# Two gate blocks of layer 2's modulation, from TensorE in the attention to VectorE in the scans

## Chip, cores and metric

One Trainium2 chip, one core. A core has five engines that run at the same time, each through its own list of instructions in order: TensorE (PE, matrix products into PSUM), VectorE (DVE), ScalarE (ACT), GpSimd (POOL) and SyncE (SP, which here only starts transfers). The profile shows the loading of a product's fixed operand as a row of its own (PEld). The metric is the time of one execution in microseconds (us); less is better. Inputs and outputs are float32.

## What is computed

Two layers on 256 latent tokens and 256 context tokens of width 2048: first two kinds of attention side by side, then a gated DeltaNet. In each, a vector `c` for the latent tokens and one, `c_ctx`, for the context tokens become a shift, a scale and a gate through the weights `w_mod`.

```python
def adaln_params(cond, w_mod, b_mod):
    return jnp.split(jax.nn.silu(cond) @ w_mod + b_mod, 3, axis=-1)

def modulate(x, gain, shift, scale):
    return rmsnorm(x, gain) * (1 + scale) + shift
...
def deltanet_layer(x, ctx, c, c_ctx, w_mod, b_mod, norm, w_in, conv_w, a_log, dt_bias, o_norm, w_out, update_ctx):
    sh, sc, gt = adaln_params(c, w_mod, b_mod)
    sh_c, sc_c, gt_c = adaln_params(c_ctx, w_mod, b_mod)
    qx, kx, vx, zx, gx, bx = deltanet_inputs(modulate(x, norm, sh[:, None], sc[:, None]) @ w_in, conv_w, a_log, dt_bias)
    qc, kc, vc, zc, gc, bc = deltanet_inputs(modulate(ctx, norm, sh_c, sc_c) @ w_in, conv_w, a_log, dt_bias)
...
    x = x + gt[:, None] * deltanet_out(o_xf + flip_t(o_xb), zx, o_norm, w_out)
    if update_ctx:
        ctx = ctx + gt_c * deltanet_out(o_cf + flip_t(o_cb), zc, o_norm, w_out)
    return x, ctx
...
        x, ctx = deltanet_layer(x, ctx, c, c_ctx, dn_w_mod[j], dn_b_mod[j], dn_norm[j], dn_w_in[j], dn_conv[j],
                                dn_a_log[j], dn_dt_bias[j], dn_o_norm[j], dn_w_out[j], update_ctx)
    return rmsnorm(x, final_norm)
```

The second layer is the last, so `update_ctx` is false there: its gate is used for the latent tokens alone, after the scans.

## The kernel before

**Modulation.** The 6144 columns of `w_mod` (2048 rows) are cut into 12 blocks of 512 columns, 4 MB each; `mods[l]` holds the result for both vectors (two samples, column 0 for `c`, column 1 for `c_ctx`). In layer 2 (`l` = 1) blocks 0 to 3 are the shift, 4 to 7 the scale, 8 to 11 the gate. Two helpers compute a block:

- `adaln` (L121) on TensorE: 16 products `pmod` (L141) of the weights `mraw` with `cond`, four at a time in different columns of the array, a copy to `macc` on VectorE (L147), four transposes `pmt` (L150), and small sums into `mods`.
- `adaln_lanes` (L161) on VectorE: for each of the 16 slices of 128 rows and each sample, a multiply-add of 128x512 into `lacc` (L175 for the first slice, L177 after it), 32 in all; then 8 small products `pml` with ones (L184) that sum over the partitions. Two accumulators, one per sample, take turns.

Both load through the buffers `mraw` of one pool, three of them at this place, 512 KB each, and `lacc` is one buffer.

**Stages.** Layer 1 runs through a first attention (neighbourhood, seven heads and an eighth later) and a latent one (eight heads), then the output projection `mm<-gx` (16 units of 48 products, L90 to L92). Up to the end of layer 1's work the order of every engine is made by a scheduler: it follows the order of the code as a priority, and starts early what is free to start. A head is `attend` (L367): scores `sp`, maximum (L389), exponential, reciprocal (L394) and scaling (L395), transposes `pt`, the split `PT` (L358), the product `po` (L365), and `goA` and `goB` (L405), whose second closes a head.

Layer 2's blocks 2, 3 and 8 are stepped through during the latent heads on TensorE (L472), block 9 after them (L495). The latter's products are kept behind the last product of the last head's projections (`issue_after`, L139). Blocks 4 to 7 follow on VectorE (L512), and 10 and 11 on TensorE at the change of layers (L522). They all pass through the same three `mraw` buffers in this order.

**The scans.** Layer 2's scans over chunks (L1220 on) run in an order written out by hand for PE, DVE and ACT: 70 steps `st` from -2 to 69. A step carries one step of the context's scan (`C`) and, six steps behind, one of the latent tokens' (`X`), and up to step 57 one weight tile of 128x1024 for the values (24 products of 512 columns). `hi` (L1125) loads weight tiles into four buffers `raw`, three ahead, and casts one on ACT (L1131); `lo` (L1134) makes the rest `wlo` on DVE (L1139). In a scan step PE makes `pks` (L1033), DVE makes `R` from it (L1037), PE makes `ptr` from R (L1045). Every second step ends, on DVE, with two conv taps (L585) in front of the next step's R; every fourth has the gated output (L1111) there too. `project` (L632) uses the gate, from step 58 on.

Of the kernel before, what the change touches and what calls it, by code (L numbers as in the profile page):

```python
# [8 lines left out]
F32 = mybir.dt.float32  # L9
F32R = mybir.dt.float32r  # L10
AF = mybir.ActivationFunctionType
ALU = mybir.AluOpType
# [4 lines left out]
KT = 16  # L17
# [9 lines left out]
def trunk_kernel(ctx: ExitStack, tc: tile.TileContext, g):  # L27
# [16 lines left out]
    def cst(name, shape, src=None):  # L44
        t = const.tile(shape, F32, name=name, tag=name)
        if src is not None:
            nc.scalar.dma_start(t, src)
        return t
# [14 lines left out]
    ab_bmod, dn_bmod = vecs[:, 56:104], vecs[:, 104:152]  # L63
    o_gain = vecs[:, 152:153]
    mods = [cst(f"mod{l}", [128, 48, 2]) for l in range(2)]
    Am = [cst(f"Am{l}", [128, KT, 2]) for l in range(2)]


    def load_raw(src, n=1024):
        raw = wp.tile([128, 1024], F32, name="raw", tag="raw", bufs=4)  # L70
        nc.sync.dma_start(raw[:, :n], src)
        return raw
# [88 lines left out]
    def adaln_lanes(l, ps, pm, tp, chunks, after=None):  # L161

        wm, bmod, gain = ((g["ab_wm"], ab_bmod, ab_gain), (g["dn_wm"], dn_bmod, dn_gain))[l]
        for ch in chunks:
# [26 lines left out]
                V.tensor_tensor(Am[l][:, f], Am[l][:, f], gain[:, f].unsqueeze(2).broadcast_to([128, 4, 2]), op=ALU.mult)  # L191
            yield

    def steps(it, n=1000):
        for _ in range(n):
            if next(it, it) is it:
                break
# [62 lines left out]
    with tc.tile_pool(name="s0", bufs=2) as tp, tc.tile_pool(name="s0p", bufs=1, space=PSUM) as ps:  # L260
        V.memset(cond, 0.0)
        A.activation(cond[:, :, 0:2], cc, AF.Silu)
        xs = ((xA, g["xT"]), (xB, g["cT"]))
        for j in range(0, KT, 4):
            for x, src in xs:
# [53 lines left out]
    with tc.tile_pool(name="ab", bufs=2, reuse_waits="tile") as tp, \  # L319
            tc.tile_pool(name="abp", bufs=2, space=PSUM, reuse_waits="tile") as ps:  # L320
        u, last_mm = NS, None
        mr = tc.alloc_tile_pool(name="mr", bufs=2)

        def later(pool, parts, after=None):
            for l, chunks, lanes in parts:
                if lanes:
                    yield from adaln_lanes(l, ps, "pm", pool, chunks, after)
                else:
                    yield from adaln(l, ps, ("pm", "pm"), pool, [(4 * ch, 4) for ch in chunks], after=after)
# [139 lines left out]
                V.tensor_tensor(ch[:, 8 + j], craw[:, j], ch[:, j].bitcast(F32), op=ALU.subtract)  # L469
        cr.release()  # L470
        mr = tc.alloc_tile_pool(name="mr2", bufs=2, reuse_waits="tile")
        ahead = later(mr, ((1, (2, 3, 8), 0),))  # L472

        rows = slice(0, 64), slice(64, 128)
        attend(*na7)
# [16 lines left out]
            attend(*o, 8 + h, None, ([qr[:, 2 * h + i] for i in range(2)], [kr[:, i] for i in range(2)]))  # L492

        steps(ahead)
        steps(later(mr, ((1, (9,), 0),), last_mm))  # L495
        pace = 0
        gx = parts_tile("gx")
        gh, gl = gx[:, 0], gx[:, 1]
# [141 lines left out]
    with tc.tile_pool(name="dn", bufs=2, reuse_waits="tile") as tp, \  # L640
# [356 lines left out]
        def load(kh, s):  # L997
            o = Head()
            o.s, o.kh = s, kh
            n = 4 if s == 0 else 2  # L1000
            o.kq, o.kt = kq[s][kh % 2], kt[s][kh % 2]
            nc.sync.dma_start(o.kq, spk[kh][:, 512 * s:512 * s + 128 * n].rearrange("p (s t) -> p s t", t=128))
            nc.sync.dma_start(o.kt, spt[kh][:, 256 * s:256 * s + 256].rearrange("p (s t) -> p s t", t=128))
            u0 = (kh % 2) * 8 + s * 4
            o.ub = zb[s][kh % 2]
            blocks(o.ub, spu[kh // 2][:, :, u0:u0 + 4])
            if s == 0:
                o.ab = zb[2][kh % 2]
                blocks(o.ab, spt[kh][:, 512:1024].rearrange("p (a u i) -> p a u i", a=2, i=64))
                o.ot = ots[kh % 2]  # L1010
            return o
# [110 lines left out]
        W += [g["dn_wo"][u][:, 1024 * c:1024 * c + 1024] for u, c in wo_order]  # L1122
        raws, wt = [], []

        def hi():  # L1125
            j = len(wt)
            if j < len(W):
                while len(raws) < min(len(W), j + 3):
                    raws.append(load_raw(W[len(raws)]))
                h = wp.tile([128, 1024], F32R, name="whi", tag="whi", bufs=3)  # L1130
                A.copy(h, raws[j])  # L1131
                wt.append([h])
# [22 lines left out]
        def nothing():  # L1155
            return iter(())
# [59 lines left out]
        outs = early()  # L1216
        GATES = {56: (0, 4, 8), 57: (12, 16), 58: (20,), 66: (24,)}
        LAG = 6
        fins = nothing()
        for st in range(-2, 64 + LAG):  # L1220
            i, n = st // 4, st % 4
# [66 lines left out]
                take(fins, 1)  # L1288
            if vals and st % 2 == 1:
                prev = cur  # L1290
            for k in GATES.get(st, ()):
                gate(k, 4)
            if st == 68:
# [146 lines left out]
```

## Time and profile before

| | us |
|---|---|
| median of 3 runs | 2491.8 |
| lowest and highest | 2489.74, 2504.61 |
| the profiled execution, from outside | 2493.04 |
| its span, from first to last instruction | 2491.2 |
| TensorE busy in the span | 2428.2 (97%) |
| VectorE busy | 1762.8 (71%) |

A row of a group or of the timeline has the line in the code, the engine, the operation, what it writes <- what it reads, the shape, xcount for the number of instructions merged, and what the engine waited for before it in brackets. Matmul times include their way through the array, so neighbours overlap. L90 to L92 are the three products of a split float32 multiplication.

The busy times by slice of a fortieth of the span, in tenths, show where VectorE is loaded; counted from 1, the latent heads lie in slices 12 to 15, the output projection in 15 to 18, the scans in 28 to 38:

```profile
PE   6999999999989999999999999999999999999998
DVE  4654678883356687856998988885777777777765
DMA  8872645542253366664665666774343333336454
```

### The profile page before, as it was taken

Reading aid. Unit: us, or ns where it says so; the run is one execution under the profiler, and the core shown is the slowest. Engines: PE = TensorE matmul, PEld = TensorE weight load, DVE = VectorE, ACT = ScalarE, POOL = GpSimd, SP = SyncE. Lnnn points to the kernel's source line nnn. Section 1 sums busy time; section 2 is a strip of 40 time slices with the busy share of each in tenths; the row PEclk is TensorE's granted clock in tenths of the full one; section 3 lists DMA queues with packets and bytes.
Section 4 is the critical chain, followed back from the end, with each engine's and each line's share of the span. In section 5 each row is a group of like instructions: output and inputs, shape, how many; then the busy total and the mean of one; then the engine's idle time right before and its main releaser. Section 6 shows DMA issues by size and latency. Waiting matters only on the chain.

```text
span 2491.2 us, 42483 instructions
## 1 busy us (share of the span) xinstructions
PE 2428.2 (97%) x16110; PEld 1963.1 (79%) x16110; DVE 1762.8 (71%) x3538; ACT 1105.6 (44%) x2446; POOL 161.1 (6%) x165
## 2 busy tenths in 40 slices
PE   6999999999989999999999999999999999999998
PEld 4557888888858878858998989987777777777787
DVE  4654678883356687856998988885777777777765
ACT  4223332333254432257565655634444544445453
POOL 0000000000000000020011101000000000012000
PEclk9999999999999999999999999999999999999999
DMA  8872645542253366664665666774343333336454
GB/s 252 282 277 87 200 154 172 169 157 84 88 187 110 102 198 204 226 210 136 195 173 158 179 178 180 204 201 108 87 116 103 115 112 98 106 100 184 148 193 141
DMA packets 254940, 397.24 MB, mean 159 GB/s; under 512 B 122257, under 2 KB 163857, under 8 KB 254609
## 3 DMA queue, kind: packets, MB, share of 16 engines
q1 hardware_dynamic: 253584, 393.00, 52.0%
q8 instruction: 127, 2.08, 0.3%
q10 hardware_dynamic: 1152, 1.54, 0.2%
q14 instruction: 77, 0.62, 0.1%
HBM read 356.94 MB, written 35.39 MB: 157 GB/s over the span
## 4 chain that ended last, share of the span: by engine, by line
PE 88%; issue 5%; DMA 3%; DVE 2%; ACT 1%; SPq 0%; POOL 0%; DVEq 0%; POOLq 0%; ACTq 0%
PE mm L90 21%; PE mm L91 20%; PE mm L92 20%; PE pks L1033 3%; PE pmod L141 3%; PE ptr L1045 2%; PE sp L365 2%; PE mm L105 2%; PE po L365 1%; DMA mraw<-dn_wm 1%; PE ptr L1078 1%; PE psu L1064 1%; PE pks L1064 1%; PE pt L398 1%; PE mm L107 1%
## 5 line engine op out<-in xcount | busy, mean ns | idle before, releaser
L90 PE MATMUL mm<-hx,whi 128*128 128x512 f32 (+1 forms) x2304 | 843.7, 366 | 2.3 <-ACT t L664 2.2
L91 PE MATMUL mm<-hx,whi 128*128 128x512 f32 (+1 forms) x2304 | 820.6, 356 | 2.5 <-issue 2.5
L92 PE MATMUL mm<-hx,wlo 128*128 128x512 f32 (+1 forms) x2304 | 819.4, 356 | 0.6 <-DVE wlo L78 0.6
L77 ACT CAST whi<-raw 128x1024 fp32r<-128x1024 f32 (+2 forms) x346 | 338.6, 980 | 701.4 <-PE mm L91 502.3
L78 DVE TENSOR_TENSOR wlo<-raw,whi 128x1024 fp32r<-128x1024 f32 (+2 forms) x346 | 394.3, 1142 | 204.3 <-ACT whi L77 198.2
L90 PEld LDWEIGHTS mm<-hx,whi 128*128 128x128 f32 x2304 | 438.8, 190 | 106.3 <-issue 27.0
L92 PEld LDWEIGHTS mm<-hx,wlo 128*128 128x128 f32 x2304 | 438.6, 190 | 65.1 <-issue 4.2
L91 PEld LDWEIGHTS mm<-hx,whi 128*128 128x128 f32 x2304 | 438.8, 190 | 61.4 <-issue 9.2
L177 DVE SCALAR_TENSOR_TENSOR lacc<-mraw,cond,lacc 128x512 f32<-128x512 f32 x300 | 208.6, 746 | 0.7 <-DMA mraw<-dn_wm 0.7
L585 DVE SCALAR_TENSOR_TENSOR acc<-cin,taps,acc 128x508 f32<-128x508 f32 (+3 forms) x256 | 187.2, 731 | 20.3 <-ACT acc L576 17.2
L105 PE MATMUL mm<-hx,whi 128*128 128x512 f32 x480 | 173.1, 404 | 0.1
L1055 DVE SCALAR_TENSOR_TENSOR vl<-ptr,egm,vh 128x128 fp32r<-128x128 f32 x224 | 64.7, 346 | 95.1 <-ACT rf L1052 37.9
L107 PE MATMUL mm<-hx,wlo 128*128 128x256 f32 x457 | 128.4, 281 | 1.3 <-DVE wlo L1139 1.2
L141 PE MATMUL pmod<-mraw,cond 128*32 128x512 f32 (+2 forms) x640 | 98.4, 508 | 28.1 <-DMA mraw<-ab_wm 18.8
L1139 DVE TENSOR_TENSOR wlo<-raw,whi 128x1024 fp32r<-128x1024 f32 x84 | 102.5, 1221 | 13.5 <-ACT whi L1131 13.4
L105 PEld LDWEIGHTS mm<-hx,whi 128*128 128x128 f32 x480 | 88.9, 188 | 24.5 <-issue 5.0
L816 DVE SCALAR_TENSOR_TENSOR outer<-L,bv,X 128x31 f32<-128x31 f32 (+15 forms) x248 | 99.4, 401 | 6.4 <-POOL X L811 0.5
L90 PE MATMUL mm<-gx,whi 128*128 128x512 f32 x256 | 100.3, 394 | 3.4 <-DVE x1B L515 2.4
L599 ACT ACTIVATE ac<-acc 128x128 f32<-128x128 f32 x160 | 37.4, 300 | 144.2 <-DVE acc L585 144.1
L91 PE MATMUL mm<-gx,whi 128*128 128x512 f32 x256 | 100.4, 392 | 0.5 <-DVE gx L503 0.5
L92 PE MATMUL mm<-gx,wlo 128*128 128x512 f32 x256 | 99.8, 391 | 0.0
L1049 ACT ACTIVATE vh<-ptr,egm 128x128 fp32r<-128x128 f32 x224 | 71.3, 374 | 57.1 <-PE ptr L1045 55.2
(301 smaller groups left out, 3648.5 us busy)
## 6 DMA issues: line engine op xcount, KB each, us to landing
raw<-dn_w SPq DMA_DIRECT2D x194, 512.0 KB
mraw<-dn_wm SPq DMA_DIRECT2D x96, 512.0 KB
mraw<-ab_wm SPq DMA_DIRECT2D x88, 512.0 KB
raw<-ab_w SPq DMA_DIRECT2D x66, 512.0 KB
raw<-dn_wo SPq DMA_DIRECT2D x64, 512.0 KB
raw<-ab_wo SPq DMA_DIRECT2D x32, 512.0 KB
raw<-ab_w SPq DMA_DIRECT2D x32, 256.0 KB
spt<-sp SPq DMA_DIRECT2D x64, 128.0 KB
```

The costliest lines, as they stand in the source:

```text
L77: A.copy(hi[:, :m], raw[:, :m])
L78: V.tensor_tensor(lo[:, :m], raw[:, :m], hi[:, :m].bitcast(F32), op=ALU.subtract)
L90: PE.matmul(ps, wh[:, c], xh[:, k0 + k, sl], start=first and k == 0, stop=False)
L91: PE.matmul(ps, wh[:, c], xl[:, k0 + k, sl], start=False, stop=False)
L92: end = PE.matmul(ps, wl[:, c], xh[:, k0 + k, sl], start=False, stop=last and k == kt - 1)
L105: PE.matmul(p2, wh[:, c], x[:, :, k0 + k], start=start, stop=stop)
L107: PE.matmul(p2[:, 0], wl[:, c], x[:, 0, k0 + k], start=False, stop=False)
L141: PE.matmul(pmod[32 * q:32 * q + 32, :m], cond[:, 4 * kg + q, :], raw[c // 1024][:, half + c % 1024:half + c % 1024 + m], start=kg == 0, s ...
L177: V.scalar_tensor_tensor(acc[:, s], raw[:, q], cond[:, k, s:s + 1], acc[:, s], op0=ALU.mult, op1=ALU.add)
L585: V.scalar_tensor_tensor(o3[:, :, i0:i1], p3[:, :, i0 + d:i1 + d], taps[:, ch, t:t + 1], o3[:, :, i0:i1], op0=ALU.mult, op1=ALU.add)
L816: V.scalar_tensor_tensor(o, L[:, rows, k:k + 1].broadcast_to([128, n, m]), bv[:, k:k + 1], X[:, k:k + 1, cols].broadcast_to([128, n, m]), ...
L1139: V.tensor_tensor(w, raws[j], h.bitcast(F32), op=ALU.subtract)
```

## The change

Blocks 8 and 9 are no longer computed by `adaln` in the attention. A new helper, `lanes`, computes them on VectorE during the scans, for the latent tokens' sample alone (`n` = 1), one weight tile of two slices per step, from step 5 to step 20; the first load is issued in step 4. Each tile takes two multiply-adds, both on the same accumulator, which lies in a free part of `room["e"]`. Its loads use the `raw` buffers of the scans' weights, so `hi` looks only two tiles ahead (`depth`) while it lasts. `cond` does not live as long as the scans, so column 0 is copied to `cond1` at the start. After each eighth tile, four products with ones sum over the partitions.

```diff
@@ -63,6 +63,7 @@
     mods = [cst(f"mod{l}", [128, 48, 2]) for l in range(2)]
+    cond1 = cst("cond1", [128, KT, 1])
     Am = [cst(f"Am{l}", [128, KT, 2]) for l in range(2)]
@@ -191,6 +192,35 @@
+    def lanes(l, chunks, acc_of, cnd, n, pt_of):
+        wm, bmod = ((g["ab_wm"], ab_bmod), (g["dn_wm"], dn_bmod))[l]
+        tiles = [(ch, t) for ch in chunks for t in range(8)]
+        load = lambda ch, t: load_raw(wm[ch, t // 2][:, t % 2 * 1024:t % 2 * 1024 + 1024])
+        ahead = load(*tiles[0])
+        yield
+        for i, (ch, t) in enumerate(tiles):
+            raw, ahead = ahead, load(*tiles[i + 1]) if i + 1 < len(tiles) else None
+            if t == 0:
+                acc = acc_of(ch)
+            for q in range(2):
+                k = 2 * t + q
+                for e in range(n):
+                    x = raw[:, 512 * q:512 * q + 512]
+                    if k == 0:
+                        V.tensor_scalar(acc[e], x, cnd[:, k, e:e + 1], None, op0=ALU.mult)
+                    else:
+                        V.scalar_tensor_tensor(acc[e], x, cnd[:, k, e:e + 1], acc[e], op0=ALU.mult, op1=ALU.add)
+            yield
+            if t == 7:
+                pt = pt_of(n)
+                for j in range(4):
+                    for e in range(n):
+                        PE.matmul(pt[:, j, e:e + 1], acc[e][:, j * 128:j * 128 + 128], ones[:, 0:1], start=True, stop=True)
+                f = slice(4 * ch, 4 * ch + 4)
+                V.tensor_tensor(mods[l][:, f, :n], pt, bmod[:, f].unsqueeze(2).broadcast_to([128, 4, n]), op=ALU.add)
@@ -260,6 +290,7 @@
         A.activation(cond[:, :, 0:2], cc, AF.Silu)
+        A.copy(cond1, cond[:, :, 0:1])
@@ -469,7 +500,7 @@
-        ahead = later(mr, ((1, (2, 3, 8), 0),))
+        ahead = later(mr, ((1, (2, 3), 0),))
@@ -492,7 +523,6 @@
         steps(ahead)
-        steps(later(mr, ((1, (9,), 0),), last_mm))
@@ -1122,10 +1152,13 @@
+        depth = 3
         def hi():
             j = len(wt)
             if j < len(W):
-                while len(raws) < min(len(W), j + 3):
+                while len(raws) < min(len(W), j + depth):
@@ -1216,6 +1249,9 @@
         LAG = 6
+        gates = lanes(1, (8, 9), lambda ch: [room["e"][:, 3072 + 512 * (ch % 2):3584 + 512 * (ch % 2)]], cond1, 1,
+                      lambda n: ps.tile([128, 4, n], F32, name="pml", tag="tr", bufs=1))
@@ -1288,6 +1324,10 @@
+            if st == 3:
+                depth = 2
+            if 4 <= st < 56:
+                depth = 2 if next(gates, 0) is None else 3
             for k in GATES.get(st, ()):
```

The order of the instructions changes at three places. Lines after the change are some 30 higher than before (L177 is L178 there, L405 is L436, L1037 is L1067).

The first is the list of PE where the last latent head is worked on, from its last projections on; before the change:

```order
L92 MATMUL mm<-cx,wlo 128x512
L141 MATMUL pmod<-mraw,cond 32x512 x5
L398 MATMUL pt<-ident,pr 128x128 x2
L141 MATMUL pmod<-mraw,cond 32x512
L365 MATMUL sp<-kT,qT 128x512
L365 MATMUL po<-PT,vt 128x256
L365 MATMUL sp<-kT,qT 128x512 x3
L365 MATMUL sp<-kr,cx 128x512 x3
L365 MATMUL sp<-kT,qT 128x512
L365 MATMUL po<-PT,vt 128x256 x11
```

and after it:

```order
L93 MATMUL mm<-cx,wlo 128x512
L396 MATMUL sp<-kT,qT 128x512 x2
L396 MATMUL sp<-kr,cx 128x512 x3
L396 MATMUL po<-PT,vt 128x256
L396 MATMUL sp<-kT,qT 128x512 x3
L396 MATMUL sp<-kr,cx 128x512 x3
L396 MATMUL po<-PT,vt 128x256 x11
L429 MATMUL pt<-ident,pr 128x128 x4
L396 MATMUL sp<-kT,qT 128x256 x3
L396 MATMUL sp<-kr,cx 128x256 x3
L185 MATMUL pml<-ones,lacc 128x1
L396 MATMUL po<-PT,vt 128x256
```

Block 9's `pmod` are gone, and `pml`, the sums of a block that VectorE computed (one of 4 to 6), now stands within the head.

The second is the list of VectorE in one of the latent heads, behind the `goB` that closes the head ahead of it; before:

```order
L405 TENSOR_TENSOR goB<-po,goB 128x256
L358 TENSOR_TENSOR vt<-pv,vt 128x512
L389 TENSOR_REDUCE mx<-sp 128x1
L358 TENSOR_TENSOR PT<-pt,PT 128x4x128
L389 TENSOR_REDUCE mx<-sp 128x1
L361 SCALAR_TENSOR_TENSOR qT<-mm,qT 128x512
L394 RECIPROCAL rc<-sm 128x1
L395 TENSOR_SCALAR pr<-pr,rc 128x256
L78 TENSOR_TENSOR wlo<-raw,whi 128x512
L358 TENSOR_TENSOR kT<-mm,kT 128x512
L147 COPY macc<-pmod 128x512
```

and after:

```order
L436 TENSOR_TENSOR goB<-po,goB 128x256
L192 TENSOR_TENSOR Am_87<-Am_87,vecs 128x8
L389 TENSOR_TENSOR vt<-pv,vt 128x512
L389 TENSOR_TENSOR PT<-pt,PT 128x4x128
L425 RECIPROCAL rc<-sm 128x1
L178 SCALAR_TENSOR_TENSOR lacc<-mraw,cond,lacc 128x512 x2
L426 TENSOR_SCALAR pr<-pr,rc 128x256
L79 TENSOR_TENSOR wlo<-raw,whi 128x1024
L420 TENSOR_REDUCE mx<-sp 128x1
L178 SCALAR_TENSOR_TENSOR lacc<-mraw,cond,lacc 128x512 x3
L389 TENSOR_TENSOR PT<-pt,PT 128x4x128
L425 RECIPROCAL rc<-sm 128x1
```

Multiply-adds of blocks 4 to 6 (L177 before, L178 now) stand between the head's own instructions; before the change none stands in the first seven latent heads.

The third is in the scans, at the end of an even step with the gated output; VectorE before:

```order
L1083 TENSOR_TENSOR rf<-rf,ptr 128x256
L585 SCALAR_TENSOR_TENSOR acc<-cin,taps,acc 128x2x254 x2
L1111 SCALAR_TENSOR_TENSOR re<-pot,ngain,re 128x512
L1037 SCALAR_TENSOR_TENSOR R<-pks,neg,vx_17131 128x128 x2
L1037 SCALAR_TENSOR_TENSOR R<-pks,neg,vc 128x128 x2
L1055 SCALAR_TENSOR_TENSOR vl<-ptr,egm,vh 128x128 x2
```

and after:

```order
L1113 TENSOR_TENSOR rf<-rf,ptr 128x256
L615 SCALAR_TENSOR_TENSOR acc<-cin,taps,acc 128x2x254 x2
L1141 SCALAR_TENSOR_TENSOR re<-pot,ngain,re 128x512
L214 SCALAR_TENSOR_TENSOR re<-raw,cond_85,re 128x512 x2
L1067 SCALAR_TENSOR_TENSOR R<-pks,neg,vx_17049 128x128 x2
L1067 SCALAR_TENSOR_TENSOR R<-pks,neg,vc 128x128 x2
L1085 SCALAR_TENSOR_TENSOR vl<-ptr,egm,vh 128x128 x2
```

The two multiply-adds of `lanes` (L214) come between the conv taps and the next step's R. On SP's queue at such a place, before:

```order
L71 DMA raw<-dn_w 128x1024
L993 DMA rc<-spt_8931 64x8x64
L995 DMA rc<-spt_8931 64x4x64
L1003 DMA rf<-spt_8932 128x256
L71 DMA raw<-dn_w 128x1024
L1002 DMA kq_16903<-spk_8917 128x256
```

and after:

```order
L72 DMA raw<-dn_w 128x1024
L1023 DMA rc<-spt_8849 64x8x64
L1025 DMA rc<-spt_8849 64x4x64
L72 DMA raw<-dn_wm 128x1024
L1033 DMA rf<-spt_8850 128x256
L72 DMA raw<-dn_w 128x1024
L1032 DMA kq_16821<-spk_8835 128x256
```

A load of the modulation's weights (`dn_wm`) stands between two loads of the scans' weights (`dn_w`), ahead of the loads of a head's keys.

## The prediction

> **What bounds the kernel now.** I read the page's first lines, then a table of windows by stage, then the chain of waits in order of time.
>
> ```profile
> span 2491.2 us, 42483 instructions
> PE 2428.2 (97%) x16110; PEld 1963.1 (79%) x16110; DVE 1762.8 (71%) x3538; ACT 1105.6 (44%) x2446; POOL 161.1 (6%) x165
> ```
>
> TensorE (PE) is busy for 97% of the span, but such a share hides stages with different limits. The windows below give, per stretch, its length and then the busy time of PE, weight loads (PEld), VectorE (DVE) and ScalarE (ACT). The first is the first latent head with what leads up to it, the second the next six heads, the third one of these six that has no modulation work in it, the fourth the last head, the fifth the output projection.
>
> ```profile
> 719.88:766.18 46.30, 44.40 (x225) 31.12 (x224) 28.16 (x57) 20.59 (x40) 0.00 (x0) 1.00 0.56 184
> 766.18:873.81 107.63, 107.63 (x615) 85.90 (x615) 65.48 (x142) 47.89 (x109) 0.00 (x0) 1.00 0.33 104
> 838.36:854.84 16.48, 16.48 (x96) 14.22 (x95) 10.60 (x24) 7.74 (x19) 0.00 (x0) 1.00 0.20 65
> 873.81:901.31 27.50, 27.04 (x134) 21.06 (x133) 25.90 (x62) 14.37 (x42) 0.00 (x0) 1.00 0.50 156
> 901.31:1066.00 164.69, 161.28 (x729) 133.80 (x730) 130.74 (x199) 40.70 (x61) 0.00 (x0) 0.99 0.68 217
> ```
>
> A plain head takes 16.48 us, PE never idle, VectorE working 10.60 of it. So PE sets the heads, and VectorE has 5.9 us to spare in each. The projection is PE's too (161.28 of 164.69).
>
> The scans come next: the chain of waits passes the same product, pks, again and again.
>
> ```profile
> 1771.61 1.45 PE pks L1033 x12
> ...
> 1810.60 1.45 PE pks L1033 x12
> ...
> 2005.52 1.45 PE pks L1033 x12
> ...
> 2044.50 1.45 PE pks L1033 x12
> ```
>
> ```profile
> 2000.00:2100.00 100.00, 100.00 (x625) 77.44 (x623) 73.15 (x191) 48.36 (x154) 7.93 (x8) 1.00 0.38 107
> ```
>
> 1810.60 − 1771.61 = 38.99 us for four steps, and 2044.50 − 2005.52 = 38.98 much later: the scans tick with PE, 9.75 us a step, and in the window above VectorE works 73.15 of 100 us. A microsecond taken from PE in the heads or put on it in the scans counts in full, unless another engine takes over as the bound.
>
> **Part 1, blocks 8 and 9 leave TensorE.** Busy time of the instructions on pmod (first two rows) and on pmt (last two), in windows around each block:
>
> ```profile
> 755.00:795.00 40.00, 5.09 (x32) 0.85 (x32) 0.69 (x1) 1.00 0.43 139
> 858.00:880.00 22.00, 7.81 (x32) 1.23 (x32) 0.69 (x1) 1.00 0.65 211
> ...
> 755.00:810.00 55.00, 0.60 (x4) 0.50 (x4) 0.19 (x1) 1.00 0.38 122
> 858.00:880.00 22.00, 0.60 (x4) 0.47 (x4) 0.00 (x0) 1.00 0.65 211
> ```
>
> PE is freed of 5.09 + 7.81 + 0.60 + 0.60 = 14.1 us, VectorE of 0.69 + 0.69 + 0.19 = 1.6. All of it lies in the heads, on the path.
>
> **Part 2, what the diff does not say.** Blocks 4 to 7 were computed on VectorE, as multiply-adds into lacc, nearly all in the output projection, since block 9 kept the mraw buffers until the last head's projections were issued. Without it the scheduler pulls them into the heads. Counted in the order of VectorE from one goB row to the next, the multiply rows (L175, L177) in the eight latent heads go from 0, 0, 0, 0, 0, 0, 0, 13 to 22, 14, 14, 14, 4, 18, 12, 15, that is 100 more.
>
> ```profile
> L177 DVE SCALAR_TENSOR_TENSOR lacc<-mraw,cond,lacc x300: 730/746/754, 280.2 to 1063.4; 128x512 f32<-128x512 f32 x150
> ...
> 911.39 2.73 DVE L177 SCALAR_TENSOR_TENSOR lacc<-mraw,cond,lacc 128x512 f32<-128x512 f32 x4
> ```
>
> One lasts 746 ns, but four in a row take 2.73 us, since each starts before the one ahead has ended: (2.73 − 0.746) / 3 = 0.66 us apart. A head with 14 of them asks VectorE for 10.60 + 14 × 0.66 = 19.8 us against PE's 16.48: the bound changes engine. Over all eight heads VectorE needs 28.16 + 65.48 + 25.90 + 100 × 0.66 − 1.6 = 183.9 us, where the stretch now takes 46.30 + 107.63 + 27.50 = 181.43. It cannot be busy throughout: the head with 4 multiplies needs 10.60 + 2.64 = 13.2 us of it, 3.2 below the plain head's 16.48, and the first stretch 28.16 + 22 × 0.66 = 42.7, some 2.4 below the 45.1 that is left of 46.30 without a quarter of block 8 (5.09 / 4). So 183.9 + 5.6 = 189.5 us, **8.1 us longer**. From below: if the order lets all multiplies hide, PE's own work is left. The sums of blocks 4 to 6 over the partitions (pml) move along with them:
>
> ```profile
> 940.88 1.68 PE pml L184 x16
> ```
>
> 44.40 + 107.63 + 27.04 − 14.1 + 3 × 1.68 = 170.0 us, with today's 2.4 us of waits 172.4, or 9.0 shorter. From above: the multiplies stand inside the softmax sequence of an engine that works in order, so each may delay what PE waits for next; wholly serial that is 181.4 − 14.1 − 1.6 + 66.0 = 231.7 us, 50 longer. I take the busy sum: the plain head's row shows 5.9 us of idle time to fill, which the serial end denies.
>
> The Trainium skill, "VectorE: DVE Perf Modes", section "The DRAIN you can't avoid", says that an operation does not start until the pipe has emptied, and that one that is not held may start earlier. By its first half the hundred would cost 74.6 us in place of 66.0, and the sum would be 8.6 us higher; by the 2.73 us row the second half holds here.
>
> **Part 3, the output projection.** Three of its four sums over partitions are gone from PE: 3 × 1.68 = **5.0 us shorter**, as PE is its bound. VectorE's 130.74 us there lose the multiplies, which gains nothing more.
>
> **Part 4, the multiplies in the scans.** For one sample there are 2 per tile, one tile a step, at the end of steps 5 to 20. Both write the same accumulator, so they do not overlap; two such rows are the conv taps (L585), 1.53 us. Rows around the end of an even step, with the products ptr that need R:
>
> ```profile
> 1771.99 1.53 DVE L585 SCALAR_TENSOR_TENSOR acc<-cin,taps,acc 128x508 f32<-128x508 f32 x2
> ...
> 1773.95 0.60 DVE L1037 SCALAR_TENSOR_TENSOR R<-pks,neg,vc 128x128 f32<-128x128 f32 x2
> ...
> 1775.60 0.61 PE L1045 MATMUL ptr<-R,ra 128*128 128x128 f32 x4
> ...
> 1781.34 0.42 DVE L1083 TENSOR_TENSOR rf<-rf,ptr 128x256 f32<-128x256 f32 x1 [1.06 <-PE ptr L1078]
> ...
> 1782.36 0.61 DVE L1037 SCALAR_TENSOR_TENSOR R<-pks,neg,ra 128x128 f32<-128x128 f32 x2 [0.60 <-PE pks L1033]
> ...
> 1782.89 0.60 DVE L1037 SCALAR_TENSOR_TENSOR R<-pks,neg,vc 128x128 f32<-128x128 f32 x2
> ...
> 1785.29 0.61 PE L1045 MATMUL ptr<-R,ra 128*128 128x128 f32 x4
> ...
> 1813.59 0.60 DVE L1037 SCALAR_TENSOR_TENSOR R<-pks,neg,vc 128x128 f32<-128x128 f32 x2
> ...
> 1814.59 0.61 PE L1045 MATMUL ptr<-R,rb 128*128 128x128 f32 x4
> ```
>
> After an even step R is done at 1774.55 and used at 1775.60, 1.05 us later. The new pair stands ahead of R in VectorE's queue, so PE waits 1.53 − 1.05 = 0.48 us. Where the gated output (L1111) is in the queue too, R is done at 1814.19 and used at 1814.59: 1.53 − 0.40 = 1.13 us. After an odd step R waits 0.60 us for pks anyway and has 1.80 us to spare: nothing. Eight even steps, three with L1111: 5 × 0.48 + 3 × 1.13 = 5.8 us. The sums over partitions are half as many for one sample: 2 × 0.84 = 1.7 us of PE. Together **7.5 us longer**. Bounds: 1.7 (all waits absorbed) and 16 × 1.13 + 1.7 = 19.8.
>
> **Part 5, SP's queue and the rest.** Sixteen loads of 512 KB leave the heads and sixteen come in the scans, so SP issues as many. There they share the four raw buffers, so the lead of the weight loads falls from three tiles to two.
>
> ```profile
> 1778.78 0.33 SPq L71 DMA_DIRECT2D raw<-dn_w  x1
> ...
> 1813.41 1.03 ACT L1131 CAST whi<-raw 128x1024 fp32r<-128x1024 f32 x1
> ...
> 895.99 8.21 DMA mraw<-dn_wm
> ...
> 2240.90 4.02 DMA re<-god
> ```
>
> The load of 1778.78 is cast at 1813.41 (the fourth cast after it): 34.6 us of lead, less two steps of 9.75 makes 15.1. Loads of that size were waited for 8.21 us in the busy projection, 4.02 in the scans: still hidden. Behind a modulation load that waits for VectorE stand kt, rf and the next weights, but what it waits for was done a step earlier. POOL gets nothing. The copy of cond1 falls on ACT, idle for 56% of the span: nothing.
>
> **Sum.** 8.1 − 5.0 + 7.5 = +10.6 us. The profiled execution took 2493.0 us, 1.2 above the median of the three runs, 2491.8; so the median should come to 2502.4, call it **2502 us**, 0.4% longer. About 1%, 24.9 us, is what a measurement of this kernel can tell from no change.
>
> **Rivals.**
> *The heads stay with PE.* VectorE's 5.9 spare microseconds and the early weights hide all multiplies: −9.0 − 5.0 + 7.5 = −6.5, 2485 us. Against it stands 19.8 above 16.48. 0.20.
> *The scans swallow the pairs.* VectorE is idle for 27 of 100 us there, and the waits are shorter than I count: 8.1 − 5.0 + 1.7 = +4.8, 2497 us. Against it: the idle time lies after R, not before. 0.08.
> *No overlap on VectorE.* With a queue that is never empty, each multiply costs its full 746 ns: 100 × 0.746 − 66.0 = 8.6 us on top of the forecast's +10.6, so +19.2 and 2511 us. This is the first half of the Trainium skill's rule in "VectorE: DVE Perf Modes"; the trace speaks against it. 0.08.
> *The softmax becomes serial*, slower by over 1%. In the heads PE's order is fixed, a late softmax row holds all behind it, and VectorE in turn waits for PE. Half-way to the serial end, (189.5 + 231.7) / 2 = 210.6 us, the heads cost 29.2 more and the sum is 29.2 − 5.0 + 7.5 = +31.7, 2524 us. It decides from some 204 us on, where heads with 14 multiplies last over 22 us. For it: multiplies stand between maximum and reciprocal. Against it: a head of the first attention carries such rows already, VectorE 33.87 of 38.88 us busy and PE still never idle:
>
> ```profile
> 418.25:457.13 38.88, 38.88 (x200) 32.92 (x199) 33.87 (x61) 12.46 (x22) 0.00 (x0) 1.00 0.53 174
> ```
>
> 0.14.
> *Weights come late in the scans.* Where a load takes over 15.1 us each step waits; at 17 us, 16 × 1.9 = 30.4 more than the forecast, 2533 us. Twice the longest wait shown: 0.03.
>
> **Chances and range.** The forecast has the rest, 0.47, with its own range from 2496 to 2510. For 8 in 10 the range runs from 2484, where the first rival ends, to 2522, which leaves out half of the serial case and the late weights. Faster by over 1% (below 2467) is out of reach of every case: 0.01. Slower by over 1% (above 2516.7): the serial case mostly and the late weights, 0.16. Within 1%: 0.83.
>
> **What would show it.** In the profile after: goB rows of the heads with 14 multiplies about 19.8 us apart, with PE now waiting there for VectorE's rows; if they stay at 16.5, part 2 is wrong. The projection about 5 us shorter. In the scans the distance of 38.99 us grows by about 1.6 to 1.9 for steps 5 to 20, with PE's waits in front of ptr and released by R; after step 21 it is 38.99 again. Weight casts that wait for a DMA would overthrow part 5. The forecast as a whole is wrong if the heads take under 180 or over 204 us.

## The result, and the profile after

| | before | after |
|---|---|---|
| median (7 runs each) | 2492.38 us | 2509.79 us |
| lowest and highest | 2489.74, 2504.61 | 2507.82, 2513.91 |
| the profiled execution | 2493.04 us | 2509.56 us |
| its span | 2491.2 us | 2507.7 us |

The ratio is 1.0064, with a 95% interval of 1.0047 to 1.0082: 0.6% longer, a small difference, but the interval lies clear of 1. The forecast was 2502 us, 10.6 longer; the medians stand 17.4 apart.

The page's first lines, after the change:

```profile
span 2507.7 us, 42402 instructions
PE 2429.8 (97%) x16054; PEld 1965.6 (78%) x16054; DVE 1776.0 (71%) x3566; ACT 1107.9 (44%) x2449; POOL 156.3 (6%) x165
```

Almost nothing moves in the totals. The totals hide the change; the table of windows shows it. Columns as before: the stretch and its length, then the busy time of PE, PEld, VectorE (DVE), ScalarE, GpSimd, then the granted clock, the DMA share and GB/s. The first row of the kernel after is the first latent head with what leads up to it, the second the four heads behind it, the third one of these four (14 multiplies), the fourth the next two, the fifth the last head, the sixth the projection up to the first product of block 10.

```profile
720.49:776.56 56.07, 51.99 (x250) 37.15 (x249) 43.19 (x85) 23.43 (x46) 0.00 (x0) 0.97 0.56 183
776.56:850.65 74.09, 68.97 (x402) 59.20 (x400) 67.26 (x143) 31.64 (x72) 0.00 (x0) 1.00 0.38 122
814.15:832.90 18.75, 16.62 (x94) 14.04 (x94) 18.75 (x38) 8.01 (x18) 0.00 (x0) 1.00 0.46 142
850.65:891.62 40.97, 36.03 (x189) 29.92 (x190) 40.97 (x85) 17.66 (x45) 0.00 (x0) 0.92 0.48 153
891.62:916.84 25.22, 22.25 (x109) 18.29 (x107) 24.27 (x56) 9.97 (x27) 0.00 (x0) 0.99 0.39 125
916.84:1079.70 162.86, 161.57 (x711) 133.12 (x711) 69.51 (x96) 42.00 (x63) 0.00 (x0) 0.97 0.46 146
```

The same last stretch in the kernel before, up to the same product:

```profile
901.31:1069.33 168.02, 164.61 (x758) 137.12 (x758) 133.23 (x204) 42.16 (x63) 0.00 (x0) 0.99 0.68 219
```

What to see: in a head with 14 multiplies VectorE now works 18.75 of 18.75 us and PE 16.62. Before, PE was never idle there and VectorE had 5.9 us to spare. The bound has changed engine. The eight heads took 719.88 to 901.31 = 181.43 us and now take 720.49 to 916.84 = 196.35, **14.9 longer**; the projection is **5.2 shorter** (168.02 to 162.86).

In the scans PE has a wait that it did not have. Totals of PE's waits between 1750 and 1910 us, the scan steps with multiplies (the engine, what it waited for: us in total, times, the longest); the kernel before has no such line in these steps:

```profile
PE ptr L1075 <- DVE R L1067: 1.8, 3, 0.6
```

From the first pks to the last the scans take 664.5 us in place of 656.3, **8.2 longer**, so these three waits are only part of it. What lies between the projection and the scans is 2.3 us shorter (632.3 to 630.1), but this stretch, whose code hardly differs, took from 625.0 to 634.0 in the eleven profiles of this study, so that is no effect of the change. Together +14.9 − 5.2 + 8.2 − 2.3 = +15.6, of the 16.5 by which the span grew; 0.6 of what is left lies ahead of the heads.

### The profile page after: what moved, and what is told of

The parts are those of the page before. It is cut to its first block, busy times and chain, and to the rows that moved or that the text cites. A ratio compares the mean times of both kernels' runs of the same rounds, so it can differ in the third digit from the quotient of the medians.

```text
span 2507.7 us, 42402 instructions
## 1 busy us (share of the span) xinstructions
PE 2429.8 (97%) x16054; PEld 1965.6 (78%) x16054; DVE 1776.0 (71%) x3566; ACT 1107.9 (44%) x2449; POOL 156.3 (6%) x165
## 4 chain that ended last, share of the span: by engine, by line
PE 85%; issue 5%; DVE 4%; DMA 3%; ACT 2%; SPq 0%; POOL 0%; DVEq 0%; POOLq 0%; ACTq 0%
PE mm L91 21%; PE mm L92 20%; PE mm L93 20%; PE pks L1063 3%; PE pmod L142 3%; PE ptr L1075 2%; PE mm L106 2%; PE sp L396 2%; DMA mraw<-ab_wm 1%; PE ptr L1108 1%; PE po L396 1%; PE psu L1094 1%; DMA mraw<-dn_wm 1%; PE mm L108 1%; PE pks L1094 1%
## 5 line engine op out<-in xcount | busy, mean ns | idle before, releaser
L178 DVE SCALAR_TENSOR_TENSOR lacc<-mraw,cond,lacc 128x512 f32<-128x512 f32 x300 | 211.2, 740 | 0.0
L142 PE MATMUL pmod<-mraw,cond 128*32 128x512 f32 (+2 forms) x576 | 89.0, 506 | 29.8 <-DMA mraw<-ab_wm 18.5
L1172 DVE TENSOR_TENSOR wlo<-raw,whi 128x1024 fp32r<-128x1024 f32 x84 | 102.5, 1220 | 12.7 <-ACT whi L1164 12.7
```

The lines of the kernel that those rows point to most:

```text
L142: PE.matmul(pmod[32 * q:32 * q + 32, :m], cond[:, 4 * kg + q, :], raw[c // 1024][:, half + c % 1024:half + c % 1024 + m], start=kg == 0, s ...
L178: V.scalar_tensor_tensor(acc[:, s], raw[:, q], cond[:, k, s:s + 1], acc[:, s], op0=ALU.mult, op1=ALU.add)
L1172: V.tensor_tensor(w, raws[j], h.bitcast(F32), op=ALU.subtract)
```

## The experiments

Each is the kernel after with one edit, unless said otherwise. Ratios are to the kernel before on the same chip. "Heads", "projection" and "scans" are the stretches measured above: 196.4, 162.9 and 664.5 us in the kernel after, 181.4, 168.0 and 656.3 before.

| run | time, us | ratio (95%) | heads | projection | scans |
|---|---|---|---|---|---|
| multiplies held behind the heads | 2485.63 | 0.9978 (0.9966 to 0.9989) | 165.0 | 169.2 | 664.2 |
| the scans' part alone | 2500.53 | 1.0030 (1.0019 to 1.0041) | 184.2 | 167.5 | 664.5 |
| the removal alone | 2499.32 | 1.0031 (1.0020 to 1.0043) | 193.7 | 163.0 | 656.1 |
| pairs at odd steps only | 2502.46 | 1.0047 (1.0030 to 1.0063) | 193.9 | 162.6 | 657.5 |
| pairs at even steps only | 2515.72 | 1.0104 (1.0086 to 1.0122) | 195.4 | 163.0 | 670.2 |
| held, and odd steps | 2479.34 | 0.9961 (0.9946 to 0.9977) | 166.1 | 169.2 | 657.2 |
| half the multiplies | 2486.71 | 0.9985 (0.9972 to 0.9998) | 181.2 | 157.6 | 664.1 |
| held behind the first head | 2505.32 | 1.0063 (1.0048 to 1.0078) | 190.8 | 162.9 | 664.3 |
| a buffer of their own | 2544.48 | 1.0215 (1.0192 to 1.0239) | 221.3 | 163.5 | 664.5 |

### The two parts, each alone

The scans' part alone: blocks 8 and 9 go back to TensorE.

```diff
-        ahead = later(mr, ((1, (2, 3), 0),))
+        ahead = later(mr, ((1, (2, 3, 8), 0),))
...
         steps(ahead)
+        steps(later(mr, ((1, (9,), 0),), last_mm))
         pace = 0
```

> Blocks 8 and 9 stay on TensorE in the attention, and the multiplies in the scans are done besides (the two blocks of the one sample are computed twice). Theory A (the two parts of the change add up): heads 181.4 and projection 168.0 as before the change, the scans 8.2 us longer, so 2500 to 2502 us. Rival: the scans' +8.2 us comes out of what the attention left (order, clock); then within 3 us of the kernel before, 2490 to 2495.

Measured 2500.53 us. The scans take 664.5 us, the same as in the kernel after, and the heads 184.2, near those of the kernel before. Of the 2.8 us between them 2.6 lie in the first stretch (48.9 in place of 46.3), where the granted clock was 0.97 here and 1.00 there.

The removal alone: no `gates` in the scans, and `depth` stays 3.

> Blocks 8 and 9 are gone from the attention and nothing comes in the scans, so the gate of the first eight tiles of the output is left out (set to 0). Theory A: heads 196 us and projection 163, as in the kernel after, the scans as before the change: 2492 + 14.9 - 5.2 - 2.3 = 2499 to 2503 us: taking 32 matmul groups off TensorE alone makes the kernel longer. Rival: work that is left out can't cost; 2484 or less, and the kernel after's loss is all in the scans.

Measured 2499.32 us. This kernel leaves two blocks out, so it does less than the kernel before, and is 0.3% slower (interval 1.0020 to 1.0043): the scans are as before (656.1), the projection is 5 us shorter, and the heads are 12 us longer. 0.30% and 0.31% add up to 0.61%; the whole change has 0.64%. Within intervals of 0.1 to 0.2% each, the parts add up.

The heads need a word on their spread. In four profiles (the kernel after, this run, and the two runs below with pairs at odd or even steps only) VectorE and PE have the same order of instructions in the heads, and the eight took 196.4, 193.7, 193.9 and 195.4 us. All of the difference lies in the first stretch: 56.1, 53.4, 53.7 and 55.2. The seven heads behind it took 140.2 or 140.3 in each. The first stretch of this run, in two parts:

```profile
720.51:748.50 27.99, 24.86 (x112) 15.45 (x111) 17.81 (x35) 12.47 (x21) 0.00 (x0) 1.00 0.62 206
748.50:773.90 25.40, 24.52 (x140) 20.89 (x139) 25.40 (x52) 10.95 (x25) 0.00 (x0) 1.00 0.55 175
```

The granted clock over the first stretch was 1.00 in the two shorter profiles and 0.97 in the two longer ones. So 2 to 3 of the 14.9 us by which the heads grew go with the clock, and not with the multiplies.

### The heads: multiplies, or loads and order?

The multiplies of blocks 4 to 7 are issued only after the last head's goB. Their loads, and all else, stay free to come early.

```diff
-                        for s in range(2):
+                        with tc.issue_after(hold) if hold else nullcontext():
+                            for s in range(2):
...
-                V.tensor_tensor(go[s][:, h], po[:, s * S:(s + 1) * S], go[s][:, h], op=ALU.mult)
+                last_go = V.tensor_tensor(go[s][:, h], po[:, s * S:(s + 1) * S], go[s][:, h], op=ALU.mult).ins
...
-                ahead, pace = later(mr, ((1, (4, 5, 6, 7), 1),), last_mm), 1
+                ahead, pace = later(mr, ((1, (4, 5, 6, 7), 1),), last_mm, last_go), 1
```

> Theory A (the latent heads became VectorE's when the multiplies of blocks 4 to 7 moved into them): with those multiplies issued only after the last head's goB, no head carries any; the stretch of the eight latent heads falls from 196.4 us to about PE's floor, 172 to 175. The projection then holds all 128 multiplies, VectorE needs about 59 + 128 x 0.66 = 144 us there, less than its 162.9, so it stays at 163 to 166. Sum against the kernel after: some 21 us less, about 2487 us in a time, 0.2% under the kernel before. Rival B (the loads that come earlier, or the changed PE order, hold the heads): the loads still come early, so the heads stay at 190 to 196 and the time at about 2508. Rival C (the multiplies only move their cost): heads 173, projection 175 or more, time 2498 or more.

Windows of this run: four plain heads, all eight heads, and the projection.

```profile
784.46:850.20 65.74, 65.74 (x378) 56.90 (x377) 42.43 (x92) 30.91 (x73) 0.00 (x0) 1.00 0.18 57
719.03:884.07 165.04, 161.54 (x876) 131.91 (x875) 108.65 (x242) 81.10 (x188) 0.00 (x0) 0.99 0.26 85
884.07:1053.28 169.21, 167.96 (x782) 140.26 (x780) 142.01 (x219) 42.84 (x64) 0.00 (x0) 1.00 0.69 226
```

PE is busy for every microsecond of the plain heads again, and the eight heads take 165.0 us, 31 less than in the kernel after and 7 below the floor I had expected. Two things have left them besides the multiplies: the three sums over partitions, which that floor held (5.0), and 22 products of the projection, which the kernel after starts within the heads (0.23 us apart, 5.0 in all). Both are back in the projection, at 169.2 a miss (expected 163 to 166). It takes only 6.3 us more than in the kernel after and not 10; its granted clock was 1.00 in place of 0.97. All 128 multiplies now lie there, VectorE works 142.01 of 169.21 us, and PE still sets the pace. Where the line between the two stretches is drawn does not touch their sum, 334.2 us in place of 359.2. The rival that the loads or PE's order hold the heads falls, and so does the one that the cost only moves: 2485.63 us (expected 2487) is 0.2% under the kernel before.

Half the multiplies, with all loads:

```diff
-                        for s in range(2):
+                        for s in range(1 if l == 1 and ch > 3 else 2):
...
```

> The kernel after, but blocks 4 to 7 are multiplied for the first sample alone (its sums are used for the second too, whose own shift and scale are left out); all loads stay. Theory A (VectorE's time bounds the heads): 64 multiplies in the heads in place of 114 to 118, VectorE's need falls by some 30 us to under PE's floor, and the eight latent heads take 172 to 178 us in place of 196; time about 2488. Rival B (loads or PE order): heads 190 or more, time 2505 or more.

The first stretch, and the seven heads behind it:

```profile
720.89:774.27 53.38, 49.66 (x242) 36.03 (x241) 38.32 (x76) 22.09 (x43) 0.00 (x0) 0.97 0.63 210
774.27:902.11 127.84, 123.62 (x709) 105.72 (x708) 108.98 (x242) 60.28 (x147) 0.00 (x0) 1.00 0.48 153
```

The time came as expected (2486.71, expected 2488), the heads not quite: 181.2, expected 172 to 178. The seven heads are PE's again (123.62 of 127.84 busy). The first stretch stays long, with 16 multiplies in it in place of 22. That the time agreed is luck: the projection took 157.6 us, 5.2 less than in the kernel after, which I had not counted. The fourth block's sums had left it too (1.7), and its granted clock was 1.00 in place of 0.97.

### The first stretch

To see what lengthens it, the multiplies were held only until the first latent head's goB (the edit of the run with all multiplies held, with `last_go` taken at `h == 8`).

> The multiplies of blocks 4 to 7 are issued only after the first latent head's goB; the other heads carry 96 of them. Theory A (the first stretch took 56.1 us because 22 multiplies came in its last 27 us and none in its first 29): the first stretch takes 45 to 47 us, and the seven heads after it 140 us as in the kernel after, since VectorE is as full there: 185 to 188 in place of 196.4, time about 2499. Rival (the first stretch is longer through the loads or the order on PE): first stretch 54 or more, time 2506 or more.

The kernel after, its first stretch cut where the multiplies begin (749.4):

```profile
720.49:749.40 28.91, 25.75 (x106) 15.06 (x105) 16.03 (x29) 12.01 (x20) 0.00 (x0) 0.94 0.57 181
749.40:776.56 27.16, 26.24 (x146) 22.09 (x145) 27.16 (x57) 11.42 (x27) 0.00 (x0) 1.00 0.55 185
```

This run, cut at the same place, and its second head with 18 multiplies:

```profile
720.03:748.50 28.47, 24.90 (x112) 15.45 (x111) 17.24 (x32) 12.48 (x21) 0.00 (x0) 1.00 0.61 200
748.50:766.59 18.09, 18.09 (x109) 15.71 (x108) 10.90 (x26) 8.32 (x19) 0.00 (x0) 1.00 0.27 94
...
766.59:789.91 23.32, 22.09 (x124) 18.62 (x123) 23.32 (x48) 10.96 (x25) 0.00 (x0) 1.00 0.43 136
```

The first 28 to 29 us are the same in both: VectorE idles for 11 to 13 of them, and there is nothing it could multiply yet. In the kernel after, SP issues the first load of block 4 at 744.37, as the last products of block 3 start (744.3 to 744.8), and the first multiply at 749.4 waits 0.3 us for it. After that the kernel after has VectorE busy 27.16 of 27.16 us, and this run has PE busy 18.09 of 18.09. So the first stretch went from 56.1 to 46.6 as expected, by taking the multiplies out; against the profiles with a full clock in that stretch (53.4 and 53.7) the difference is 7. The time did not follow: 2505.32, expected 2499. The seven heads now hold 96 multiplies and take 144.2 us in place of 140.3, the second head alone 23.32. The saving is partly handed on, since VectorE stays the bound there.

Then the opposite: let the multiplies start earlier, with one raw buffer of their own in place of a share in three.

```diff
-                    raw = tp.tile([128, 2, 512], F32, name="mraw", tag="mraw", bufs=3)
+                    raw = tp.tile([128, 2, 512], F32, name="mraw", tag=("mraw", "lraw")[ch > 3], bufs=(3, 1)[ch > 3]) if l else tp.tile([128, 2, 512], F32, name="mraw", tag="mraw", bufs=3)
...
-                    yield from adaln(l, ps, ("pm", "pm"), pool, [(4 * ch, 4) for ch in chunks], after=after)
+                    yield from adaln(l, ps, ("pm", "pm"), pool, [(4 * ch, 4) for ch in chunks], bufs=2, after=after)
```

> The kernel after, but the loads of blocks 4 to 7 have one raw buffer of their own in place of a share in three (blocks 2, 3, 10 and 11 keep two), so they no longer wait for block 3 on TensorE, and one tile at a time sets the pace. In VectorE's order 11 multiplies then stand before the latent heads, 32 in their first stretch, and 65 in the seven heads behind it in place of 92. Theory A (the first stretch of the kernel after is long because its 22 multiplies can start only 29 us into it and then fill VectorE for 27 us): with 32 multiplies from the start on it takes no more than 52 us in place of 53 to 56, and the seven heads, with some 10 each, about 17.5 us and 24 for the last, 125 to 130 in place of 140; the heads 174 to 182, the time 2488 to 2495. Rival (the number of multiplies in the first stretch sets its length, wherever they stand): 10 more multiplies at 0.66 us make it 60 to 63. Unknown: what two buffers in place of three cost the blocks that stay on TensorE.

A miss: 2544.48 us, and a first stretch of 72.8 us. Waits of all engines between 719 and 930 us:

```profile
DVE lacc L178 <- DMA mraw<-dn_wm: 17.6, 13, 2.8
...
PE pmod L142 <- DMA mraw<-dn_wm: 13.1, 6, 5.7
```

Multiplies now wait 17.6 us for their loads at the head of VectorE's queue, blocks 2 and 3 wait 13.1 us for theirs on PE, and PE's granted clock was 0.91 in the first stretch and 0.93 in the seven heads. The run mixes these costs, so it decides nothing between theory and rival. Heads with 9 to 11 multiplies took 19.6 to 21.6 us, more than those with 14 in the kernel after; how much of that is the waiting for loads is not shown. Whether an early start with enough buffers would have saved the first stretch stays open.

### The scans: which steps pay?

Odd steps only, so that no pair stands between an even step's taps and the next R:

```diff
-            if 4 <= st < 56:
+            if 4 <= st < 56 and st % 2 == 1:
```

> The kernel after, with the pair of multiplies at the end of odd steps only (one tile in two steps, done by step 38). Theory A (PE waits for R only where the pair follows an even step): the scans' +8.2 us falls to the sums' 1.7 us and at most 1 more, so 6 to 7 us less than the kernel after, about 2503 us. Rival (it is the loads, the raw buffers held twice as long, or the lead of the weights): no less than the kernel after, 2509 or more, with the steps longer for twice as many steps.

Even steps only (`st % 2 == 0`):

> The kernel after, with the pair of multiplies at the end of even steps only (one tile in two steps). Theory A: sixteen even steps wait in place of eight: the scans' +8.2 us becomes 1.7 + 2 x 6.5 = 14.7, so about 6 us above the kernel after, 2514 to 2517. Rival (loads or lead of the weights): the same as with odd steps only, whatever that is.

Measured 2502.46 us with odd steps (expected about 2503) and 2515.72 with even steps (expected 2514 to 2517).

Four steps of the scans, from one weight cast `whi` to the fourth after it, in the kernels before, after, with odd steps only and with even steps only. Three of them are at the same place of the work; that of the kernel after lies four steps later, since a sum over partitions falls into the first place there:

```profile
1813.41:1852.40 38.99, 38.99 (x243) 30.25 (x243) 28.71 (x77) 18.59 (x60) 2.89 (x3) 1.00 0.37 105
```

```profile
1865.12:1905.95 40.83, 40.17 (x243) 30.57 (x243) 34.22 (x84) 18.79 (x59) 2.48 (x3) 1.00 0.53 152
```

```profile
1817.83:1856.81 38.98, 38.98 (x243) 30.23 (x243) 31.43 (x80) 18.70 (x59) 2.49 (x3) 1.00 0.44 131
```

```profile
1821.82:1862.64 40.82, 40.17 (x243) 30.59 (x243) 31.54 (x80) 18.71 (x60) 2.89 (x3) 1.00 0.43 127
```

The last two have the same work, loads and buffers: 80 VectorE rows, 31.43 and 31.54 us of them. At odd steps they cost nothing, at even steps 1.83 us per four steps. Twice as many multiplies in the kernel after (34.22 us of VectorE) cost 1.84, no more than the even ones alone. Over the whole, 8 even steps cost 664.5 − 657.5 = 7.0 us, 16 cost 12.7; the sums over partitions, which alone remain with odd steps, 657.5 − 656.3 = 1.2.

The wait itself, in the run with even steps, in order of time:

```profile
1780.69 1.53 DVE L214 SCALAR_TENSOR_TENSOR re<-raw,cond,re 128x512 f32<-128x512 f32 x2
...
1782.14 0.60 DVE L1067 SCALAR_TENSOR_TENSOR R<-pks,neg,ra 128x128 f32<-128x128 f32 x2
...
1782.55 0.56 PEld L1075 LDWEIGHTS ptr<-R,rb 128*128 128x128 f32 x4 [0.38 <-DVE R L1067]
1782.55 0.75 PE L1075 MATMUL ptr<-R,rb 128*128 128x128 f32 x4
```

The pair takes 1.53 us, R starts as it ends, and the first load of R as weights has waited 0.38 us for it. The four products then run as R's rows come, 0.75 us in place of 0.60.

This is not yet the whole price. PE's products come in the same order in both runs, so their starts can be set against each other one by one. From the third of these even steps on there are two kinds. Where the gated output stands in front of R too, the products on R start 0.78 us late and end 0.99 us late. In the other kind, as in the rows above, they end only 0.33 us late, but PE loses another 0.50 us some 3 us further on, at the products `ptr<-vh,ksp`. Their operand `vh` comes from ScalarE, which had waited for R as well, and then had a weight cast in front of `vh`; from the run with even steps:

```profile
1802.48 0.63 ACT L1071 ACTIVATE rf<-pks,neg 128x128 f32<-128x128 f32 x2 [1.06 <-DVE R L1067]
...
1802.99 1.05 ACT L1164 CAST whi<-raw 128x1024 fp32r<-128x1024 f32 x1
...
1803.93 0.64 ACT L1079 ACTIVATE vh<-ptr,egm 128x128 fp32r<-128x128 f32 x2
...
1805.59 0.18 PEld L1094 LDWEIGHTS ptr<-vh,ksp 64*128 64x128 f32 x1 [0.20 <-ACT vh L1079]
```

Among the totals of the waits from 1710 to 2350 us this run has such a line for seven steps, the kernel after for four; with odd steps only, and before the change, there is none:

```profile
PEld ptr L1094 <- ACT vh L1079: 1.4, 7, 0.2
```

### Both remedies at once

> Both edits at once: the multiplies of blocks 4 to 7 issued after the last head, and the pairs in the scans at odd steps only. Theory A (the two costs are separate): the sum of both savings, 21 + 6.5 us under the kernel after, about 2481 us, 0.4 to 0.5% under the kernel before. Rival (one stands in for the other): 2487 or more.

Measured 2479.34 us (expected about 2481), ratio 0.9961 (0.9946 to 0.9977): the two costs are separate, their savings add up, and this version is faster than both kernels, by 0.4% against before.

## Why the prediction was right, and where it was off

The direction and the mechanism came out as forecast: the time grew by under 1%, because the multiplies of blocks 4 to 7 moved into the heads and made VectorE their bound, and because pairs in front of R delay PE. The sum was 6.8 us too small against the medians, nearly all of it in one term; in the other two terms errors of opposite sign partly cancel, so that they came so close is in part luck.

**Part 1 and the floor.** Shown. With the multiplies away, heads and projection take 165.0 + 169.2 = 334.2 us against 349.4 before, 15.2 less; the forecast for that case (the rival "The heads stay with PE") was 9.0 + 5.0 = 14.0 less.

**Part 2, heads, forecast +8.1, measured +14.9.** This is the mis-sized term. The change of bound was right: 18.75 us for a head with 14 multiplies (forecast 19.8), fully busy on VectorE. Two errors lay in the sum of 189.5 us, of opposite sign. VectorE's busy time was put at 183.9 and measured 43.19 + 67.26 + 40.97 + 24.27 = 175.7: a multiply among other work added less than the 0.66 us of the row of four, (18.75 − 10.60) / 14 = 0.58 in that head and (175.7 − 117.9) / 100 = 0.58 over all eight, where 117.9 is 183.9 without the 66.0 for the multiplies. And its idle time was put at 5.6 and measured 196.35 − 175.7 = 20.7, of which 12.9 in the first stretch, where I had counted 2.4, and 6.8 in the four heads behind it, where I had counted 3.2. The step that failed is that VectorE works throughout a stretch unless the stretch holds too few multiplies to fill it: I set demand against the length of the whole stretch, where the multiplies can only begin half-way, because their buffers are still with block 3. In the profile before, the same place could have been read from its parts: VectorE worked 28.16 of 46.30 us there, and not evenly.

That the first stretch's excess is the multiplies' was shown by holding them: 46.6 to 48.7 us in three profiles, in place of 53.4 to 56.1 in four with 22 of them. The clock adds to both, and like has to be set beside like. At a granted clock of 1.00 it took 46.3 and 46.6 us without multiplies and 53.4 and 53.7 with 22. At 0.96 or 0.97 it took 47.5 to 48.9 without, 53.4 with 16, and 55.2 and 56.1 with 22. So 22 multiplies cost about 7 us there and 16 about 5, and the lower clock went with 1 to 2.7 us, a term that the sum did not have.

**Part 3, projection, forecast −5.0, measured −5.2.** Right in the sum, with two terms beside it that cancel. PE's busy time fell by only 3.0 us (164.61 to 161.57), where the three sums alone are 5.0; the granted clock was 0.97 in place of 0.99, which is worth at most 3 us of 163. PE's idle time fell by 2.1 (168.02 − 164.61 = 3.4 before, 162.86 − 161.57 = 1.3 after). VectorE's 64 us less there bought nothing, as said.

**Part 4, scans, forecast +7.5, measured +8.2.** The place was right: even steps pay, odd ones don't. Both prices of the wait for R were some 0.15 us too high: 0.33 in place of 0.48, and 0.99 in place of 1.13 where the gated output is in the queue too. The slack had been taken to the products at 1775.60, `ptr<-R,ra`; the first load that needs R, for `ptr<-R,rb`, starts earlier, at 1774.94, but needs only R's first row, and that was done by 1773.78. What the forecast left out is the second wait of the plain even steps, 0.50 us for `vh` from ScalarE, which also stands behind R. So a plain step cost 0.83 in all, and 0.99 + 0.83 = 1.82, of the 1.83 measured over four steps. The pairs came to 7.0 us (forecast 5.8). The sums over partitions cost 1.2 (forecast 1.7).

**Part 5, nothing for loads and the rest.** Right for the loads: no weight cast waited for a DMA in the scans, and with odd steps only, with the same loads as with even ones, the scans are 1.2 us over those before.

**The rivals.** "The heads stay with PE" needs the multiplies out of the heads; that was made by hand and gave what it said. "The scans swallow the pairs" is what odd steps alone do. "No overlap on VectorE" asked for 0.746 us per multiply; 0.58 was measured. "The softmax becomes serial" was to begin at 204 us for the heads; they took 196.4. But its mechanism is there in part. Totals of PE's waits between 749 and 917 us in the kernel after; from 766 to 901 before the change this view has no line at all:

```profile
PE sp L396 <- ACT pr L423: 5.3, 4, 1.6
PE mm L91 <- DVE qT L392: 1.8, 4, 0.7
PE sp L396 <- ACT kT L388: 1.5, 1, 1.5
...
```

And of ScalarE's, between 719 and 930 us:

```profile
ACT pr L423 <- DVE mx L420: 5.2, 5, 2.2
```

PE waits for the exponential `pr`, and that for its maximum on VectorE. The second wait alone is no sign: before the change ScalarE waited 19.1 us for the maximum (720 to 901 us), and PE had no such wait. With the multiplies held behind the heads the view of PE's waits from 766 to 884 us has one wait left, of 0.8 us.

## What to carry to other kernels

Taking work off the busiest engine can free a buffer or an order that held other work back: look at what the scheduler will pull forward, and hold it where it is if its new engine has less room there. Before filling an idle engine, set its spare time against the work by sections short enough to show when that work can start, not by whole stages. In a fixed order, filler belongs behind the row that another engine waits for: the same pairs cost 0 at odd steps and 0.8 to 1.0 us each at even ones. The slack has to be followed past the first consumer: in the plain even steps more than half of the price came 3 us later, through an engine that had waited for the same row.

## What the runs showed of the hardware

Short waits can be followed by a lower clock. In the kernel after, windows of 2 us around 852 us:

```profile
850.00:852.00 2.00, 1.10 (x5) 0.60 (x5) 2.00 (x5) 0.59 (x2) 0.00 (x0) 1.00 0.76 219
852.00:854.00 2.00, 0.90 (x3) 0.37 (x2) 2.00 (x5) 1.05 (x3) 0.00 (x0) 1.00 0.83 307
854.00:856.00 2.00, 1.79 (x5) 1.45 (x6) 2.00 (x5) 0.00 (x0) 0.00 (x0) 0.67 0.01 2
856.00:858.00 2.00, 2.00 (x6) 1.51 (x6) 2.00 (x7) 0.00 (x0) 0.00 (x0) 0.50 0.01 2
```

PE was half busy in the first 4 us, with no single wait over 1.5 us, and got 0.67 and 0.50 of its clock in the next 4, although it had work again. At half the clock its products of 512 columns start 0.43 us apart, at the full clock 0.23:

```profile
856.57 0.63 PE L91 MATMUL mm<-cx,whi 128*128 128x512 f32 x1
856.99 0.63 PE L92 MATMUL mm<-cx,whi 128*128 128x512 f32 x1
...
858.19 0.39 PE L92 MATMUL mm<-cx,whi 128*128 128x512 f32 x1
858.42 0.39 PE L93 MATMUL mm<-cx,wlo 128*128 128x512 f32 x1
```

The two heads from 850.65 to 891.62 ran at a mean clock of 0.92. The Trainium skill, "TensorE: Matmul & The Clock Gate", section "What's actually happening", has the clock fall after an idle window of about 3.4 us; here it fell after one that was only half idle. No run isolates this as the cause.

What a lower clock costs depends on what bounds the stretch. These two heads lost nothing to it: VectorE was busy for 40.97 of 40.97 us, and the same two heads took 40.96 to 40.97 us in the three other profiles with this order, at a mean clock of 0.88, 0.88 and 0.92. In the projection, which is PE's, the clock of 0.97 showed in PE's busy time, and in the first stretch it went with 1 to 2.7 us. The sum of the prediction had no term for either.
